# Attention softmax of a hybrid encoder trunk: logits and their minimum in one VectorE instruction, the mask added to the gates, 1/sum on VectorE, v transposed in another bank

## The chip, the cores and the metric

One core of one Trainium2 chip runs the whole program. The metric is the device time of one execution in microseconds (us), lower is better. The profile is of one execution, taken by the hardware profiler; its engines are PE (TensorE matmul; PEld is its weight load), DVE (VectorE), ACT (ScalarE), POOL (GpSimd) and SP (the queue that issues most of the transfers).

## What is computed

Two layers of a hybrid block run over 512 prompt tokens and 32 sample tokens. Each layer normalises x, multiplies it by one large input matrix, feeds three branches (a convolution module, retention, and forgetting attention, "FoX"), merges them with gates, and ends with a convolutional feed-forward block. The part that is changed is the attention:

```python
def fox_block(q, c_q, pos_q, k, v, c_k, pos_k):
    s = jnp.einsum('bthd,bshd->bhts', q, k) * (DH_FOX ** -0.5)
    bias = transpose(c_q)[..., :, None] - transpose(c_k)[..., None, :]   # cumulative log of the forget gate
    mask = pos_k[None, :] <= pos_q[:, None]
    s = jnp.where(mask[None, None], s + bias, -jnp.inf)
    p = jax.nn.softmax(s, axis=-1)
    return jnp.einsum('bhts,bshd->bthd', p, v)
```

There are 8 heads of 64. The prompt's 512 queries go in four blocks of 128; block qb sees (qb + 1) * 128 keys, the last 128 of them under a triangular mask. The sample's 32 queries see 256 cached keys and their own 32. The term c_q is the same for a whole row, so it drops out of a softmax over that row.

## The kernel before

**Matrix products.** Activations lie transposed (channels on partitions, 544 tokens along the row). A product by a large weight is three passes of matmuls of 272 columns (high part by high, high by low, low by high), accumulated in `acc` (pool psA, two buffers): L310, in `gemm`. One `slot` is one output tile of 128 channels: 48 such matmuls and an eviction by a callback, mostly `R_norm.evict` (L399, VectorE, `acc` times the norm). A weight block comes over the SP queue as `raw` (L195), is rounded into `hi` (L203, ScalarE), copied negated into `lo` (L206, ScalarE), and a GpSimd transfer that adds (L207) makes `lo` the remainder.

**What is woven in.** In the middle of a `gemm`, after 2/8, 4/8 and 6/8 of its passes, hooks call work that was put off (`later`), one step of the generators in `side` and some steps of those in `extra` (`tick`). `conv_side` is in `extra`: the depthwise convolution, one VectorE instruction of 574 columns a step (L486, then L488, 27 per channel tile, four tiles a layer), and products of ScalarE (L491) summed on GpSimd (L495). `fox_side` is in `side`: attention, 34 items (2 of the sample, then 32 of the prompt: head pairs, four query blocks each, even head then odd head). At step k item k computes its scores and softmax, item k-3 its transposes, item k-5 its product with v. A scheduler then orders each engine's instructions by when it reckons them ready, with earlier program text first, so that an engine's queue is not the program's order; on the chip each queue runs in the order so fixed.

**One item of the prompt.** Scores (L747, TensorE) of an even head and its mate go into the two buffers of psS at once. `c` is the row of cumulative gates of the head, broadcast to 128 partitions by a transfer (`ck`, L672, three buffers). L753 (VectorE) makes c - c_q - scores out of PSUM, L754 adds the mask on the last 128 columns, L680 takes the row's minimum, L682 (ScalarE) the exponential with its row sum, L684 (VectorE) the reciprocal, L685 (ScalarE) multiplies by it. Then four-fold transposes into the one buffer of psT (L761), their eviction (L763, ScalarE), and the products with v into the one buffer of psO (L779). The sample's two items do the same with L694, L700, L705, L706 and L712 to L731.

**Before it.** Just ahead of attention stand the slots of q (four), k (four) and v (four, `v_done`), then those of the retention's q and k, whose rotation reads a copy by transfers (L808), then L811 (GpSimd), L812 (VectorE) and L813 (GpSimd). q and k are normalised two slots after their product: `head_mean` multiplies by a block matrix into the two buffers of psS (L341, L342), and `rsqrt` reads them (L353 on ScalarE, L357 on VectorE). `v_done` transposes v, also two slots later: four transposes into a buffer of psS (L625), one into psT (L627), both evicted by ScalarE (L628, L629). The same callback serves the retention's v later in the layer, where the retention itself uses psO (L890).

## Time and profile before

| | |
|---|---|
| device time, median of 3 runs | 1995.84 us (1991.99 to 1999.47) |
| the profiled execution | 1999.15 us, of which the span from first to last instruction is 1997.0 us |
| PE busy | 1951.2 us (98%) |
| DVE busy | 950.5 us (48%) |
| ACT busy | 1062.5 us (53%) |
| POOL busy | 425.3 us (21%) |
| mean granted TensorE clock | 0.991 |

Each row of a group below is one line of the profile. In lists of instructions the columns are: line, engine, operation, output<-input by the program's names, output<-input shape, number; then busy time in us, the mean of one in ns; then the engine's idle time just before them in us and what released it. In a timeline a line begins with its start and its length in us, and the idle time before it stands in square brackets.

### The profile page before, as it was taken

The page shows a single profiled execution, that of the slowest core. Times are in us where ns is not written, and L with a number is a line of the kernel's source. Part 1 is how long each engine was busy: PE and PEld are TensorE (multiplying, and loading weights), DVE is VectorE, ACT ScalarE, POOL GpSimd, SP SyncE. Part 2 cuts the span into 40 slices and gives each one's busy share as a digit, 9 for nine tenths or more (in the row PEclk, how much of TensorE's full clock was granted, in tenths as well). Part 3 has the DMA queues.
Part 4 walks back from the last instruction along what each step waited for, and adds up shares of the span by engine and source line. Part 5 has one row for each costly group of instructions (what it writes and reads, how often), then busy time and mean ns, then how long its engine had stood idle before and what let it go on. Part 6 is the DMA issues. An engine that isn't in the chain of part 4 may idle for free.

```text
span 1997.0 us, 37750 instructions
## 1 busy us (share of the span) xinstructions
PE 1951.2 (98%) x15832; PEld 1909.6 (96%) x15832; DVE 950.5 (48%) x1641; ACT 1062.5 (53%) x1462; POOL 425.3 (21%) x580
## 2 busy tenths in 40 slices
PE   7999999999999999999999998999999999999999
PEld 6999889999999999999999987999999999999999
DVE  4377978555234330233224869784543343303330
ACT  5475664476455543454555666636654554434442
POOL 2142422121111221122112334121211122112211
PEclk8999999999999999999999999999999999999999
DMA  7786646567787787787987775556778877777786
GB/s 226 173 186 163 155 106 135 133 153 164 177 218 175 173 179 174 174 176 176 209 205 160 191 172 127 127 122 146 152 169 197 197 175 174 178 173 177 174 184 141
DMA packets 105717, 337.91 MB, mean 169 GB/s; under 512 B 17628, under 2 KB 19276, under 8 KB 105164
## 3 DMA queue, kind: packets, MB, share of 16 engines
q0 software_dynamic: 41760, 152.06, 45.6%
q1 hardware_dynamic: 63788, 183.44, 27.8%
q8 instruction: 124, 2.03, 0.4%
q14 instruction: 45, 0.37, 0.1%
HBM read 321.11 MB, written 9.89 MB: 166 GB/s over the span
## 4 chain that ended last, share of the span: by engine, by line
PE 80%; issue 6%; DVE 6%; ACT 2%; DMA 2%; POOL 2%; SPq 1%; DVEq 0%; POOLq 0%; ACTq 0%
PE acc L310 75%; DVE w L488 3%; DMA lo<-in_wpack_dram 1%; PE s L747 1%; DMA w<-q 1%; PE o L779 1%; DVE w L754 1%; PE t L761 1%; DVE w L753 1%; POOL lo L207 1%; DMA w<-cscr 0%; DVE mn L680 0%; POOL w L377 0%; ACT lo L206 0%; PE s L866 0%
## 5 line engine op out<-in xcount | busy, mean ns | idle before, releaser
L310 PE MATMUL acc<-q,hi 128*128 128x272 f32 x9344 | 1791.3, 291 | 12.7 <-ACT q L328 7.6
L310 PEld LDWEIGHTS acc<-q,hi 128*128 128x128 f32 x9344 | 1478.4, 190 | 27.1 <-ACT q L328 8.7
L310 PE MATMUL acc<-q,lo 128*128 128x272 f32 x4672 | 1352.2, 290 | 5.7 <-DMA lo<-in_wpack_dram 5.4
L310 PEld LDWEIGHTS acc<-q,lo 128*128 128x128 f32 x4672 | 884.4, 190 | 6.8 <-DMA lo<-in_wpack_dram 6.3
L203 ACT ACTIVATE hi<-raw 128x1024 fp32r<-128x1024 f32 (+1 forms) x293 | 309.8, 1057 | 655.5 <-PE acc L310 654.0
L207 POOL DMA_DIRECT2D lo<-in_wpack_dram x290 | 251.7, 868 | 1264.6 <-ACT lo L206 1174.9
L206 ACT ACTIVATE lo<-hi 128x1024 fp32r<-128x1024 f32 x290 | 305.1, 1052 | 4.4
L488 DVE SCALAR_TENSOR_TENSOR w<-w,par 128x574 f32<-128x574 f32 x208 | 198.4, 954 | 3.8
L1177 DVE TENSOR_TENSOR q<-acc,q 128x544 f32<-128x544 f32 x32 | 23.2, 725 | 218.6 <-PE acc L310 218.6
L399 DVE TENSOR_TENSOR w<-acc,R 128x544 f32<-128x544 f32 x94 | 67.7, 720 | 120.2 <-PE acc L310 118.4
L1136 DVE TENSOR_TENSOR w<-acc,R 128x32 f32<-128x32 f32 x44 | 8.5, 192 | 154.6 <-PE acc L310 154.1
L1144 DVE SCALAR_TENSOR_TENSOR w<-w,par 128x546 f32<-128x546 f32 x44 | 34.7, 788 | 83.5 <-ACT w L1143 83.5
L1146 ACT ACTIVATE w<-w 128x546 f32<-128x546 f32 x44 | 29.1, 662 | 70.5 <-DVE w L1145 70.5
L682 ACT ACTIVATE w<-w,mn 128x128 f32<-128x128 f32 (+4 forms) x68 | 37.7, 555 | 31.4 <-DVE mn L680 29.0
L326 DVE TENSOR_TENSOR q<-w,q 128x544 fp32r<-128x544 f32 x44 | 31.9, 725 | 33.7 <-ACT q L325 33.7
L335 DVE TENSOR_TENSOR wr<-w,wr 128x544 fp32r<-128x544 f32 x24 | 26.5, 1104 | 42.7 <-ACT wr L334 42.7
L495 POOL TENSOR_TENSOR w<-w 128x574 f32<-128x574 f32 x24 | 40.1, 1670 | 19.8 <-ACT w L491 19.2
L357 DVE SCALAR_TENSOR_TENSOR w<-s,w 128x272 f32<-128x272 f32 (+1 forms) x60 | 23.6, 435 | 43.4 <-ACT w L354 42.9
L1016 DVE SCALAR_TENSOR_TENSOR w<-w,acc 128x544 f32<-128x544 f32 x32 | 23.0, 720 | 43.6 <-PE acc L310 43.3
L685 ACT ACTIVATE w<-w,rs 128x128 f32<-128x128 f32 (+4 forms) x68 | 37.4, 554 | 9.6 <-DVE rs L684 9.2
L753 DVE SCALAR_TENSOR_TENSOR w<-ck,CM,s 128x128 f32<-128x128 f32 (+3 forms) x64 | 34.3, 536 | 13.4 <-PE s L747 13.4
L811 POOL TENSOR_TENSOR w<-w,cst 128x544 f32<-128x544 f32 x16 | 27.1, 1693 | 56.4 <-DMA w<-q 56.4
(203 smaller groups left out, 1434.7 us busy)
## 6 DMA issues: line engine op xcount, KB each, us to landing
raw<-in_wpack_dram SPq DMA_DIRECT2D x291, 512.0 KB, 3.4
lo<-in_wpack_dram POOLq DMA_DIRECT2D x290, 512.0 KB, 5.5
w<-in_x_dram SPq DMA_DIRECT2D x16, 272.0 KB, 5.2
out_dram<-w SPq DMA_DIRECT2D x16, 272.0 KB, 4.7
w<-q SPq DMA_DIRECT2D x64, 68.0 KB, 4.0
ck<-cscr SPq DMA_DIRECT2D x16, 256.0 KB, 4.2
xn<-q SPq DMA_DIRECT2D x8, 272.0 KB, 5.3
w<-xn SPq DMA_DIRECT2D x8, 272.0 KB, 5.8
```

The source lines that it names most:

```text
L203: act(hi[:, sl], self.raw[u][:, sl], AF.Copy)
L206: act(lo[:, sl], hi[:, sl].bitcast(F32), AF.Copy, scale=-1.0)
L207: nc.gpsimd.dma_start(lo[:, sl], wpack[u][:, sl], accum_op=ALU.add)
L310: mm(acc[:, h, :HN], w, half(x, h), start=(i == 0 and j == 0), stop=(i == n - 1 and j == len(passes) - 1))
L326: vtt(lo, src, hi.bitcast(F32), op=ALU.subtract)
L399: vtt(two(out), acc, two(self.R), op=ALU.mult)
L488: stt(c, u[:, k : k + CO], pcol(w + k), c, op0=ALU.mult, op1=ALU.add)
L495: gtt(p, p, t, op=ALU.add)
L682: act(L[:, :n], L[:, :n], AF.Exp, scale=-1.0, bias=mn, accum_out=sm)
L685: act(L[:, :n], L[:, :n], AF.Copy, scale=rs)
L753: stt(L[:, :n], c[:, :n], CM[:, h, qb : qb + 1], p[:, :n], op0=ALU.subtract, op1=ALU.subtract)
L1144: stt(c, a[:, 1 : 1 + FO], pcol(w + 1), c, op0=ALU.mult, op1=ALU.add)
```

## The change

Five things are altered, in `v_done`, `softmax`, `s_scores` and `p_scores`. (1) The attention's v is transposed into psO's buffer (the retention's v still into psS), and `vs` has one buffer in place of two. (2) The scale of q is negated, so that scores come out negative. (3) A new helper `ck_diag` adds the mask to the 128 gates of the diagonal block on GpSimd, into four buffers `cm`; it is called for the item at hand and for the same head's next query block, and at the end of a head pair for the next pair. (4) L753, L754 and L680 become one or two `tensor_tensor_reduce`: sum of gates and scores, and its minimum, on the columns before the diagonal block and then on the diagonal block with the first minimum as start; c_q is dropped. The sample's items keep their instructions. (5) The product with 1/sum goes from ScalarE (L685) to a VectorE `tensor_scalar`, for sample and prompt. The loads of `ck` are asked for earlier in the program.

```diff
-        def v_done(vt, vs, j, out):
+        def v_done(vt, vs, j, out, bank):
...
-                    t = psS_t()
+                    t = bank()
...
-        nc.vector.tensor_scalar(gq8, pcol(P_GQ), 0.125, None, op0=ALU.mult)
+        nc.vector.tensor_scalar(gq8, pcol(P_GQ), -0.125, None, op0=ALU.mult)
...
-        fvs = spool.tile([P, 512], F32, tag="vs", name="vs")
+        fvs = spool.tile([P, 512], F32, tag="vs", name="vs", bufs=1)
         for j in range(4):
-            slot(rhs, v_done(fv, fvs, j, o_fv[l]))
+            slot(rhs, v_done(fv, fvs, j, o_fv[l], psO_t))
...
+            def ck_diag(h, qb):
+                if h < 8 and (h, qb) not in ckm:
+                    t = wpool.tile([P, P], F32, tag="cm", name="cm", bufs=4)
+                    gtt(t, ck(h)[:, qb * P : (qb + 1) * P], cmask, op=ALU.add)
+                    ckm[h, qb] = t
+                return ckm.get((h, qb))
...
-            def softmax(L, n):
-                mn = spool.tile([P, 1], F32, tag="mn", name="mn", bufs=4)
-                nc.vector.tensor_reduce(mn, L[:, :n], axis=AX.X, op=ALU.min)
+            def softmax(L, n, mn=None):
+                if mn is None:
+                    mn = spool.tile([P, 1], F32, tag="mn", name="mn", bufs=4)
+                    nc.vector.tensor_reduce(mn, L[:, :n], axis=AX.X, op=ALU.min)
...
-                act(L[:, :n], L[:, :n], AF.Copy, scale=rs)
+                nc.vector.tensor_scalar(L[:, :n], L[:, :n], rs, None, op0=ALU.mult)
...
-                stt(L[:, :n], cks[g], cqs[:, g : g + 1], p[:, :n], op0=ALU.subtract, op1=ALU.subtract)
+                stt(L[:, :n], cks[g], cqs[:, g : g + 1], p[:, :n], op0=ALU.subtract, op1=ALU.add)
...
-                stt(L[:, :n], c[:, :n], CM[:, h, qb : qb + 1], p[:, :n], op0=ALU.subtract, op1=ALU.subtract)
-                vtt(L[:, n - P : n], L[:, n - P : n], cmask, op=ALU.add)
-                softmax(L, n)
+                m = ck_diag(h, qb)
+                if qb < 3:
+                    ck_diag(h, qb + 1)
+                mn = [spool.tile([P, 1], F32, tag="mn" + x, name="mn", bufs=4) for x in "ab"]
+                at = BIG
+                for x, o, e, t in ((c[:, : n - P], 0, n - P, mn[0]), (m, n - P, n, mn[1])):
+                    if e > o:
+                        nc.vector.tensor_tensor_reduce(L[:, o:e], x, p[:, o:e], 1.0, at, ALU.add, ALU.min, t)
+                        at = t
+                softmax(L, n, mn[1])
+                if qb == 1 and h % 2 and h < 7:
+                    ck(h + 1)
+                if qb == 3 and h % 2 == 0 and h < 6:
+                    ck(h + 3)
+                if qb == 3 and h % 2 and h < 7:
+                    ck_diag(h + 1, 0)
+                    ck_diag(h + 2, 0)
```

## Rows read from the trace of the kernel before

**Rows 1.** The first part of the profile's page: busy time of each engine, share of the span, instructions.

```profile
span 1997.0 us, 37750 instructions
PE 1951.2 (98%) x15832; PEld 1909.6 (96%) x15832; DVE 950.5 (48%) x1641; ACT 1062.5 (53%) x1462; POOL 425.3 (21%) x580
```

**Rows 2.** The waits of the PE alone, over the span: line, what it waited for, us in total, number, longest.

```profile
PE s L747 <- DVE w L753: 5.8, 4, 3.0
...
PE t L761 <- ACT w L763: 5.1, 4, 1.9
PE s L625 <- DVE w L357: 4.2, 2, 2.1
...
PE t L712 <- ACT w L717: 1.6, 2, 0.9
PE s L694 <- DVE w L705: 0.8, 2, 0.4
```

**Rows 3.** Stretches by time (us from the span's start): length, then busy time of PE, PEld, DVE, ACT, POOL with the number of instructions, then the granted TensorE clock (1.00 is full), the DMA share and GB/s. The first five are the stretches right behind a wait of the PE; the last is one in which VectorE is full.

```profile
147.50:151.50 4.00, 4.00 (x20) 4.00 (x21) 3.96 (x7) 1.39 (x3) 1.01 (x3) 0.57 1.06 274
1133.30:1137.30 4.00, 4.00 (x23) 4.00 (x24) 3.96 (x7) 1.39 (x3) 0.96 (x2) 0.65 1.05 274
181.20:185.60 4.40, 4.38 (x21) 4.01 (x22) 2.24 (x6) 2.34 (x8) 2.44 (x3) 0.61 0.82 142
256.90:260.50 3.60, 3.55 (x17) 3.55 (x18) 3.60 (x7) 0.49 (x1) 0.99 (x1) 0.55 0.74 179
1209.20:1212.80 3.60, 3.58 (x15) 2.89 (x16) 3.60 (x9) 2.39 (x7) 1.96 (x1) 0.55 0.96 207
...
214.00:262.00 48.00, 42.62 (x343) 37.42 (x343) 47.45 (x86) 29.61 (x63) 21.52 (x15) 0.96 0.57 132
```

**Rows 4.** Timeline of the first layer in the slots of v, by engine: first VectorE (two lines hold several instructions of the convolution), then the first v's transposes on TensorE and their eviction on ScalarE; last, two slots of 48 matmuls from the chain of waits, as a measure of an undisturbed slot (start, length, what).

```profile
141.42 5.67 DVE L488 SCALAR_TENSOR_TENSOR w<-w,par 128x574 f32<-128x574 f32 x2
147.01 0.78 DVE L357 SCALAR_TENSOR_TENSOR w<-s,w 128x272 f32<-128x272 f32 x2
149.07 0.71 DVE L399 TENSOR_TENSOR w<-acc,R 128x544 f32<-128x544 f32 x1
150.40 6.14 DVE L488 SCALAR_TENSOR_TENSOR w<-w,par 128x574 f32<-128x574 f32 x6
156.46 0.72 DVE L399 TENSOR_TENSOR w<-acc,R 128x544 f32<-128x544 f32 x1
...
147.50 0.66 PE L625 MATMUL s<-cst,w 128*128 128x128 f32 x4 [2.10 <-DVE w L357]
...
148.19 0.60 ACT L628 ACTIVATE q<-s 128x512 f32<-128x512 f32 x1 [1.82 <-PE s L625]
...
97.97 6.01 PE acc L310 x48
104.48 6.00 PE acc L310 x48
```

**Rows 5.** VectorE's instructions of the softmax and of the convolution over the whole span, by shape.

```profile
L753 DVE SCALAR_TENSOR_TENSOR w<-ck,CM,s 128x128 f32<-128x128 f32 x16 | 5.4, 337 | 2.2 <-PE s L747 2.2
L753 DVE SCALAR_TENSOR_TENSOR w<-ck,CM,s 128x256 f32<-128x256 f32 x16 | 7.5, 472 | 4.1 <-PE s L747 4.1
L753 DVE SCALAR_TENSOR_TENSOR w<-ck,CM,s 128x384 f32<-128x384 f32 x16 | 9.6, 602 | 4.8 <-PE s L747 4.8
L753 DVE SCALAR_TENSOR_TENSOR w<-ck,CM,s 128x512 f32<-128x512 f32 x16 | 11.8, 735 | 2.2 <-PE s L747 2.2
L754 DVE TENSOR_TENSOR w<-w,cst 128x128 f32<-128x128 f32 x64 | 29.2, 456 | 0.8
L680 DVE TENSOR_REDUCE mn<-w 128x1 f32<-128x128 f32 x16 | 4.5, 279 | 0.3
...
L680 DVE TENSOR_REDUCE mn<-w 128x1 f32<-128x512 f32 x16 | 10.8, 677 | 0.1
L486 DVE TENSOR_SCALAR w<-w,par 128x574 f32<-128x574 f32 x8 | 4.6, 570 | 0.0
```

**Rows 6.** Single lines of the program: number, shortest/median/longest in ns, first and last start.

```profile
L639 DVE TENSOR_SCALAR gq<-par x2: 154/154/154, 5.4 to 31.2; 128x1 f32<-128x1 f32 x2
L754 DVE TENSOR_TENSOR w<-w,cst x64: 266/284/1495, 175.7 to 1270.0; 128x128 f32<-128x128 f32 x64
L682 ACT ACTIVATION_READ_ACCUMULATOR w<-w,mn x68: 184/188/192, 172.6 to 1274.3; 128x1 f32 x68
L685 ACT ACTIVATE w<-w,rs x68: 385/528/726, 173.3 to 1275.5; 128x128 f32<-128x128 f32 x16, 128x256 f32<-128x256 f32 x16, 128x384 f32<-128x384 f32 x16, 128x512 f32<-128x512 f32 x16
```

**Rows 7.** One group of GpSimd's instructions, in the stretch from 174.6 to 265 us alone.

```profile
L811 POOL TENSOR_TENSOR w<-w,cst 128x544 f32<-128x544 f32 x8 | 13.4, 1672 | 29.6 <-DMA w<-q 29.6
```

**Rows 8.** Timelines of VectorE (first three lines: one mask addition, and the first and last logits of the prompt in the first layer) and of GpSimd (the other two), at the same clock of the trace.

```profile
211.15 1.28 DVE L754 TENSOR_TENSOR w<-w,cst 128x128 f32<-128x128 f32 x1
...
175.27 0.35 DVE L753 SCALAR_TENSOR_TENSOR w<-ck,CM,s 128x128 f32<-128x128 f32 x1 [0.70 <-PE s L747]
...
285.46 0.73 DVE L753 SCALAR_TENSOR_TENSOR w<-ck,CM,s 128x512 f32<-128x512 f32 x1
...
178.06 1.90 POOL L811 TENSOR_TENSOR w<-w,cst 128x544 f32<-128x544 f32 x1 [7.40 <-DMA w<-q]
...
210.93 1.36 POOL L813 TENSOR_TENSOR q<-q,w 128x544 f32<-128x544 f32 x1
```

More of the change, by code (lines that the diff above doesn't have):

```diff
@@ L674, in ck @@
                 return ckp[h]
+            ckm = {}
+            def ck_diag(h, qb):
[4 more added lines that the diff above has]
+                return ckm.get((h, qb))
             yield
-            def softmax(L, n):
-                mn = spool.tile([P, 1], F32, tag="mn", name="mn", bufs=4)
-                nc.vector.tensor_reduce(mn, L[:, :n], axis=AX.X, op=ALU.min)
+            def softmax(L, n, mn=None):
+                if mn is None:
+                    mn = spool.tile([P, 1], F32, tag="mn", name="mn", bufs=4)
+                    nc.vector.tensor_reduce(mn, L[:, :n], axis=AX.X, op=ALU.min)
                 sm = spool.tile([P, 1], F32, tag="sm", name="sm", bufs=4)
@@ L1031, in branch @@
                     if m == 0:
-                        rvt.extend((vtile(), spool.tile([P, 512], F32, tag="vs", name="vs")))
-                    slot(rhs, v_done(rvt[0], rvt[1], m, None))
+                        rvt.extend((vtile(), spool.tile([P, 512], F32, tag="vs", name="vs", bufs=1)))
+                    slot(rhs, v_done(rvt[0], rvt[1], m, None, psS_t))
                 elif kind == "r":
```

## The prediction, made before the changed kernel ran

> **What bounds the kernel now.** The page comes first: TensorE is busy for 98% of the span, no other engine for much over half [rows 1]. So nothing done on VectorE, ScalarE or GpSimd shortens the kernel in itself; only time in which TensorE waits, or runs at its lower clock, can come back. The list of TensorE's waits says how much that is and which part of it this change touches [rows 2]: scores that wait for the logits to be read out of psS (5.8 us), transposes that wait for psT's eviction (5.1), v's transposes that wait for psS (4.2), and the sample's items (1.6 and 0.8): 17.5 us.
>
> To that belongs what follows a wait. The stretches behind the five longest stops show a granted clock of 0.55 to 0.65 [rows 3], the engine being at the lower of its two levels (1.2 in place of 2.4 GHz) for most of them. At clock g a stretch of t us loses (1 - g) t: 1.7 and 1.4 us behind v's two waits, 1.7 behind the sample's, 1.6 and 1.6 behind two of attention's, 8.0 us in all. Together 25.5 us of 1997 hang on waits that the change touches. That is the most it can give by this way, and it is 1.3%.
>
> Behind attention's waits stands VectorE. It is busy 47.45 of 48 us in the stretch of the first layer where they fall [rows 3], and the second layer's is alike; the convolution's instructions are packed into whatever other work leaves, six in a row between two evictions of v [rows 4], so a logit that is ready still queues.
>
> **v into psO.** What goes is the wait for psS, which k's last normalisation holds until its two reads (L357, from 147.01) are through [rows 4]; in front of them a pair of convolution instructions took 5.67 us. psO has no reader at that time: its next user, the sample's product with v, stands behind all four slots of v. So 4.2 us of waiting and 3.1 us of clock are at stake, 7.3. What is late next: with 2.1 us won the last v slot is done at about 157.1 (the transposes begin at 145.4 and take 0.66, three quarters of a slot of 6.0 us follow, then one whole slot at a pitch of 6.5 [rows 4]), while the third v is evicted only from 156.46 to 157.18 [rows 4], and the slot after needs that buffer. The v before it is evicted by 149.78, ahead of the 150.6 at which its buffer is wanted. I keep 0.4 us a layer for that: **-6.5 us**. That four v tiles now share one buffer costs nothing: a slot lies between two of them and the eviction takes 0.60 us [rows 4]. vs in one buffer costs nothing either: the sample is first in attention and the retention's first write comes when attention's 110 us [rows 8] are over; without that distance it would be one wait for an eviction.
>
> **The sample's start.** The 0.8 us of L694 come from psS shared with v's transposes, and go with them. The 1.6 us of L712 wait for an eviction on ScalarE behind other work, L685 among it. Of these and the 1.7 us of clock behind the first I take half: **-2.4 us** with the 0.8.
>
> **Softmax on VectorE.** What is removed, from the busy times of [rows 5]: L753 34.3, L754 29.2, L680 30.6 (64 at the mean of its smallest and largest, as its time grows evenly with the columns), together 94.1 us in both layers. What is added: the new instruction reads the same columns, in pieces. No row shows it; its nearest is L753, which also adds a row in SBUF to PSUM. In 16 items of each size that is 128; 128+128; 256+128; 384+128 columns: four pieces of 128 and one each of 128, 256, 384, at 337, 337, 472, 602 ns, thus 16 x 2.76 = 44.1 us. If the minimum is read out by an instruction of its own, as ScalarE's row sum is (188 ns [rows 6]), 112 of these add 21 us; L680 writes its minimum with no such row, and I take zero. The product with 1/sum: between 154 ns for one column [rows 6] and 570 for 574 [rows 5] lie 246, 340, 430 and 520 ns for the four sizes, 24.6 us; the other end is one column at a time as in L680, 30.6 us. The reciprocal stays. So VectorE is relieved by 94.1 - 44.1 - 24.6 = 25 us, 19 with the slow product, about nothing with readouts as well.
>
> **The mask on GpSimd.** 64 additions of 128 columns are new. L811 has 544 in 1.67 us [rows 7]; by columns that is 0.39, and with a fixed part like that of VectorE's L680 (279 ns for 128 where a quarter of 677 is 169 [rows 5]) 0.50: 25 to 32 us on an engine that is busy for 21% [rows 1]. But it meets VectorE: L754 takes 0.28 us in the median and up to 1.5 [rows 6], and the one of 1.28 us starts at 211.15 while GpSimd's L813 runs from 210.93 to 212.29 [rows 8]. L753, with one operand in PSUM, shows no such spread between its sizes [rows 5]. The Trainium skill, page "SBUF — State Buffer", section "Who interferes with whom", has this as an exclusive lock: a VectorE instruction with two SBUF inputs and a GpSimd instruction that reads SBUF exclude each other, and a tensor_scalar in its two-port mode excludes any GpSimd work. The trace agrees on the first with those two rows (1.28 against 0.28 us); on the second no run here shows anything yet. By the rule the new logits are out of it and the 64 additions and 68 products are in it, which is the second rival below.
>
> I let half of the additions' time fall on VectorE. The 32 items of a layer take 110 us [rows 8], 3.5 each, so the 48 us of [rows 3] hold some 13: 13 x 0.39 (25 us over 64) = 5.1 us of relief, less 13 x 0.45 / 2 = 2.9, so 2.2 us net. VectorE's lateness there is what the 5.8 us of score waits measure, 2.9 a layer; 2.2 a layer of it goes: -4.4.
>
> **ScalarE.** L685 goes, 68 at a median of 528 ns, 36 us over both layers [rows 6]. In 13 items that is 6.9 us off a queue in which L763, the eviction that transposes wait for, stands behind it. Of its 5.1 us I take half, -2.5; the other half waits for VectorE through the exponential. The 3.2 us of clock behind these waits I leave where they are, since a remaining short wait has lowered the clock too (0.91 us did at 181.2) [rows 2, 3]. Attention's part is **-6.9 us**.
>
> **Edits at nothing.** The sign of q's scale is one instruction on one column. The broadcasts of ck are as many as before, asked for earlier; where one waits for its buffer it now stands ahead of rotation copies and weight loads on SP, for at most the one item whose logits release it, 3.5 us. Weights are asked for three blocks ahead (`ahead`), which covers it; without that cover each of 8 such loads could put off a slot by it.
>
> **Sum.** -6.5 - 2.4 - 6.9 = -15.8 us. Against the profiled execution (1999.15 us, 2.15 of it outside its span) that is 1983.4; that execution lies 3.3 above the median of the runs, and against the median it is 1980.0. I forecast 1980 us. About 0.5%, 10 us, is what a measurement of this kernel can tell from no change: the line lies at 1985.9.
>
> **Rivals.** *All waits go.* VectorE's relief of 25 us and ScalarE's of 36 are larger than what is waited for, so the queues may empty: 25.5 us, 1970. Against it: VectorE is full because convolution work is moved up into its gaps, and that will fill new gaps as well. 0.10.
>
> *VectorE stays full.* The additions on GpSimd shut out the products and the convolution as L813 shut out L754, and for their whole length: 64 x 0.45 = 29 us at most, as much as the relief of 19 to 25. Readouts of the minimum would do the same. Then attention's waits stay and only v's 6.5 and the 0.8 us of the sample go: -7.3, about 1988 to 1989, no change that can be told. For it speaks the 5.67 us of two convolution instructions in [rows 4]; against it that L754, which collides today, goes. 0.25.
>
> *The mask comes late* (slower). GpSimd's queue is in order, and L811 sits at its head waiting for a rotation's copy: 29.6 us in eight times, once 7.4 [rows 7, 8]. An addition that is queued behind it waits that, 1.9 for L811 and 1.4 for L813, up to 10.7 us; its lead is two items, 7.1 us. It is then up to 3.6 us late, say 2.5, and behind it stand the logits on VectorE, psS and the next scores on TensorE. Of 16 rotations six eat the whole gain; with ten it is 25 - 16 = +9 us, 2005. Against it: additions depend only on ck, which lies there long before, so they are likely put ahead. 0.13.
>
> *No effect at all*, if every wait only changes its name: 1996, 0.02.
>
> **How the numbers follow.** The forecast has 0.50, by itself from 1974 (-22) to 1987 (-9, v's part and the start alone). Of its chance 0.40 lies below 1985.9 and 0.10 within the line. All waits gone: 0.10 faster. VectorE full: 0.05 faster, 0.20 within. Late mask: 0.11 slower, 0.02 within. No effect: 0.01 within, 0.01 slower. Faster 0.55, same 0.33, slower 0.12. The range from 1969 to 1999 holds the first rival's 1970 and the no-effect case; the slower rival and the ends of the unknown costs beyond it are left out, some 0.15 to 0.2.
>
> **What would show it.** Right: v's transposes with no wait and the full clock behind them (the old places are 147.5 and 1133.3 us); no L685 on ScalarE; VectorE's softmax at 69 us in place of 94; score and transpose waits together at 4 to 5 us. The forecast is wrong if new instructions on 128 columns take clearly more than 0.34 us, if a readout row follows them, if the convolution's mean of instructions rises, or if VectorE idles in front of logits with GpSimd named as releaser.

## The result: 2008 us in place of 1994, slower by 0.6%

The changed kernel takes 2008.1 us (median of 4 runs, 2005.6 to 2010.5), the kernel before 1993.9 beside it: a ratio of 1.0063, 95% interval 1.0043 to 1.0084. The forecast of 1980, and the sign, were wrong. The profiled execution took 2007.24 us.

The first part of its page answers to [rows 1]:

```profile
span 2005.3 us, 37930 instructions
PE 1953.3 (97%) x15832; PEld 1909.1 (95%) x15832; DVE 947.1 (47%) x1741; ACT 1031.5 (51%) x1394; POOL 461.6 (23%) x644
```

ScalarE has lost 31 us and GpSimd gained 36, as planned. VectorE, which was to lose 25, has lost 3.4.

The waits of the PE over the span (line, what it waited for, us in total, times, longest) answer to [rows 2]:

```profile
PE acc L310 <- DMA lo<-in_wpack_dram: 11.5, 3, 5.3
PE s L758 <- DVE mn L772: 11.0, 6, 5.5
...
PE t L787 <- ACT w L789: 6.9, 8, 2.4
```

The 4.2 us of v's transposes and the 2.4 of the sample's start are gone from the list. But scores wait 11.0 us where 5.8 were, transposes 6.9 where 5.1 were, and two new waits, for the low part of a weight, stand in the slots of v (3.29 and 2.94 us; the old one, of 5.4 us, is elsewhere). All rows of the list together are 47.4 us, where they were 41.0.

Stretches behind the longest new waits, in the columns of [rows 3]:

```profile
152.50:157.00 4.50, 4.47 (x23) 4.47 (x24) 4.36 (x7) 0.74 (x2) 0.84 (x1) 0.62 1.02 224
231.00:236.00 5.00, 4.44 (x16) 3.69 (x17) 3.57 (x13) 1.85 (x5) 0.79 (x2) 0.52 0.46 125
1143.00:1147.50 4.50, 4.33 (x19) 4.33 (x20) 4.39 (x6) 0.91 (x3) 0.88 (x1) 0.50 1.03 217
```

As before, the granted clock is low behind these waits (0.50 is the lower of its two levels, 1.2 GHz, for a whole stretch), so such a wait costs more than its own length.

**The slots of v.** The timeline of GpSimd, and the PE's wait in it:

```profile
139.52 1.76 POOL L682 TENSOR_TENSOR cm<-ck,cst 128x128 f32<-128x128 f32 x2 [3.50 <-DMA ck<-cscr]
141.25 1.95 POOL L495 TENSOR_TENSOR w<-w 128x574 f32<-128x574 f32 x1
143.16 1.88 POOL L682 TENSOR_TENSOR cm<-ck,cst 128x128 f32<-128x128 f32 x2
144.99 0.87 POOL L207 DMA_DIRECT2D lo<-in_wpack_dram  x1
...
148.37 1.18 POOL L207 DMA_DIRECT2D lo<-in_wpack_dram  x1
...
152.53 0.48 PE L310 MATMUL acc<-q,lo 128*128 128x272 f32 x1 [3.29 <-DMA lo<-in_wpack_dram]
```

GpSimd's queue also issues the transfers that make a weight's low part (L207). Four additions of the mask now stand ahead of them, the first after 3.50 us of waiting for the gates; the two issues come 2.2 and 1.7 us later than before, where they were at 142.78 and 146.67.

**The softmax.** VectorE's instructions by shape, which answer to [rows 5], and GpSimd's additions:

```profile
L488 DVE SCALAR_TENSOR_TENSOR w<-w,par 128x574 f32<-128x574 f32 x208 | 199.0, 957 | 3.9
L772 DVE CUSTOM_DVE_ANT_0 w<-cm,s,mn 128x128 f32<-128x128 f32 x48 | 16.3, 340 | 2.6
L696 DVE TENSOR_SCALAR w<-w,rs 128x512 f32<-128x512 f32 x16 | 11.0, 689 | 0.3
...
L772 DVE DVE_READ_ACCUMULATOR2_ANT mn<- 128x1 f32 x112 | 8.9, 80 | 0.0
L772 DVE CUSTOM_DVE_ANT_0 w<-ck,s 128x384 f32<-128x384 f32 x16 | 8.7, 543 | 4.2 <-PE s L758 4.2
...
L696 DVE TENSOR_SCALAR w<-w,rs 128x128 f32<-128x128 f32 x16 | 7.8, 484 | 0.4
...
L682 POOL TENSOR_TENSOR cm<-ck,cst 128x128 f32<-128x128 f32 x64 | 42.1, 667 | 51.8 <-DVE mn L772 30.0 <-DMA ck<-cscr 20.5 <-DVE rs L695 1.0
```

The new instruction takes 0.28 to 0.34 us for 128 columns and 0.54 for 384, 40.4 us in all, and behind each of the 112 stands a readout, a row of 80 ns (`DVE_READ_ACCUMULATOR2_ANT`) that writes the minimum. These rows add up to 8.9 us, but they lie beside other instructions: 55 of the 112 start in the same nanosecond as the instruction behind them (227.56 in the next timeline), and only 0.9 of the 8.9 us lie beside no other row of VectorE. The product takes 484 ns in the mean for 128 columns and 274 at its shortest.

**The longest stall.** VectorE, GpSimd and PE in layer 0:

```profile
227.22 0.41 DVE L772 CUSTOM_DVE_ANT_0 w<-ck,s 128x256 f32<-128x256 f32 x1
227.56 0.07 DVE L772 DVE_READ_ACCUMULATOR2_ANT mn<- 128x1 f32 x1
227.56 3.67 DVE L488 SCALAR_TENSOR_TENSOR w<-w,par 128x574 f32<-128x574 f32 x1
231.16 0.33 DVE L772 CUSTOM_DVE_ANT_0 w<-cm,s,mn 128x128 f32<-128x128 f32 x1
...
231.90 0.81 DVE L488 SCALAR_TENSOR_TENSOR w<-w,par 128x574 f32<-128x574 f32 x1
...
227.64 1.70 POOL L495 TENSOR_TENSOR w<-w 128x574 f32<-128x574 f32 x1
228.99 1.62 POOL L837 TENSOR_TENSOR w<-w,cst 128x544 f32<-128x544 f32 x1
...
231.56 1.22 PE L758 MATMUL s<-q 64*128 64x512 f32 x2 [5.54 <-DVE mn L772]
```

An item's logits are now two instructions, and the second needs the first's minimum. Between them stands here an instruction of the convolution, as it does in 14 of the 48 split items; it takes 3.67 us, with two GpSimd instructions running beside it, where the next one takes 0.81. Until the second piece has read them, the scores keep their bank (their buffer in PSUM), and TensorE stands. Before, the first instruction (L753) read all the scores, and no hold was over 0.75 us; now the 48 split items hold their bank 1.32 us in the mean and 4.27 at most, from the first piece's start to the second's end.

### The profile page after: what moved, and what is told of

It reads as the page before. It is cut to its first block, busy times and chain, and to the rows that moved or that the text cites. A ratio compares the mean times of both kernels' runs of the same rounds, so it can differ in the third digit from the quotient of the medians.

```text
span 2005.3 us, 37930 instructions
## 1 busy us (share of the span) xinstructions
PE 1953.3 (97%) x15832; PEld 1909.1 (95%) x15832; DVE 947.1 (47%) x1741; ACT 1031.5 (51%) x1394; POOL 461.6 (23%) x644
## 4 chain that ended last, share of the span: by engine, by line
PE 78%; issue 6%; DVE 5%; DMA 4%; ACT 2%; POOL 2%; SPq 1%; DVEq 0%; POOLq 0%; ACTq 0%
PE acc L310 74%; DVE w L488 2%; DMA w<-q 2%; DMA lo<-in_wpack_dram 2%; PE o L805 1%; DVE w L772 1%; DVE w L696 1%; PE s L758 1%; PE t L787 1%; SPq L834 1%; POOL lo L207 1%; DMA w<-cscr 0%; PE s L892 0%; ACT hi L203 0%; PE o L916 0%
## 5 line engine op out<-in xcount | busy, mean ns | idle before, releaser
L207 POOL DMA_DIRECT2D lo<-in_wpack_dram x290 | 251.7, 868 | 1237.6 <-ACT lo L206 1175.4
L488 DVE SCALAR_TENSOR_TENSOR w<-w,par 128x574 f32<-128x574 f32 x208 | 199.0, 957 | 3.9
L682 POOL TENSOR_TENSOR cm<-ck,cst 128x128 f32<-128x128 f32 x64 | 42.1, 667 | 51.8 <-DVE mn L772 30.0
L789 ACT ACTIVATE w<-t 128x128 f32<-128x128 f32 (+3 forms) x64 | 27.4, 428 | 31.4 <-PE t L787 25.9
L758 PE MATMUL s<-q 64*128 64x256 f32 (+2 forms) x192 | 31.1, 364 | 11.0 <-DVE mn L772 11.0
```

Of the source, the lines that this page charges most:

```text
L207: nc.gpsimd.dma_start(lo[:, sl], wpack[u][:, sl], accum_op=ALU.add)
L488: stt(c, u[:, k : k + CO], pcol(w + k), c, op0=ALU.mult, op1=ALU.add)
L682: gtt(t, ck(h)[:, qb * P : (qb + 1) * P], cmask, op=ALU.add)
L758: mm(ps[e][:, :nn], qhl[a][own, h // 2, NS + qb * P : NS + n], khl[b][own, h // 2, NS : NS + nn], start=(i == 0), stop=(i == 2))
```

## The experiments

Theories at the start: (A) the additions on GpSimd cost the time, in its queue and by shutting VectorE out; (B) the product on VectorE does; later (D) the split of the logits into two pieces does, by holding the scores' bank or by making the minimum late. Ratios are to the kernel before, run beside each; where two runs are compared in us below, it is by the difference of their ratios times 1994 us, as the kernel before ran between 1993.7 and 1995.7 beside them. An edit also lets the scheduler order the engines' queues anew. By line and shape every queue of e1 has the order of the kernel before, and the queues of VectorE, ScalarE and TensorE in e2 have that of the changed kernel; in the other runs the order of VectorE's queue, at least, has moved with the edit.

| run | us (median) | ratio, 95% interval |
|---|---|---|
| changed kernel | 2008.1 | 1.0063 (1.0043 to 1.0084) |
| e1 v alone | 1992.0 | 0.9988 (0.9977 to 0.9998) |
| e2 no additions | 2008.3 | 1.0068 (1.0054 to 1.0083) |
| e3 additions on VectorE | 2004.0 | 1.0040 (1.0025 to 1.0055) |
| e4 product on ScalarE | 2004.3 | 1.0055 (1.0035 to 1.0074) |
| e5 one piece | 1990.2 | 0.9974 (0.9965 to 0.9984) |
| e6 independent pieces | 2016.7 | 1.0115 (1.0100 to 1.0129) |
| e7 as e6, product on ScalarE | 2002.8 | 1.0049 (1.0034 to 1.0063) |
| e8 one piece, product on ScalarE | 1996.2 | 1.0000 (0.9987 to 1.0014) |
| e9 one piece, mask in place | 1994.3 | 0.9999 (0.9987 to 1.0011) |
| e10 one piece, idle second | 1986.9 | 0.9949 (0.9931 to 0.9967) |
| e11 one piece, late minimum | 1998.9 | 1.0019 (1.0007 to 1.0030) |
| e12 mask by TensorE, fp32r | 2018.9 | 1.0112 (1.0088 to 1.0135) |
| e13 changed kernel, longer lag | 2004.8 | 1.0054 (1.0034 to 1.0074) |
| e14 as e9, longer lag | 1998.8 | 1.0021 (1.0008 to 1.0034) |
| e15 mask by TensorE, bf16 | 2004.1 | 1.0043 (1.0027 to 1.0059) |
| e16 as e9, mask on VectorE | 1993.6 | 0.9997 (0.9986 to 1.0008) |
| e17 as e10, second waited for | 1996.8 | 1.0005 (0.9994 to 1.0017) |
| e18 as e11, not waited for | 1992.2 | 0.9991 (0.9981 to 1.0002) |

**e1: v's part alone.** Only `v_done` and its calls are changed; `vs` keeps its two buffers.

```diff
-                    t = psS_t()
+                    t = bank()          # psO_t in attention, psS_t in retention
```

> The kernel before with one edit: attention's v is transposed into psO. Theory A (the psS wait of 2.1 us a layer goes, but TensorE then reaches the next weight block before its remainder has landed; in the changed kernel that wait was 3.3 and 2.9 us, with GpSimd's additions ahead of the transfer, and by the old places of L207 about 1.2 us of it stays without them): 3 to 5 us faster than before, v's transposes without a wait and a wait for lo of 1 to 2 us a layer in their place. Rival (nothing takes its place): 7 us faster, no wait for lo in the slots of v. Rival (all of it is given back): no difference.

It gains 0.12% (0.02 to 0.23), about 2 us. v's wait is gone and no wait for a weight takes its place, but scores now also wait for the sample's logits. PE waits of e1:

```profile
PE t L761 <- ACT w L763: 6.9, 5, 1.9
...
PE s L747 <- DVE w L753: 4.7, 4, 1.8
...
PE s L747 <- DVE w L705: 2.9, 4, 0.8
```

**e2: no additions.** The mask on the prompt is left out.

```diff
...
-                    gtt(t, ck(h)[:, qb * P : (qb + 1) * P], cmask, op=ALU.add)
-                    ckm[h, qb] = t
+                    ckm[h, qb] = ck(h)[:, qb * P : (qb + 1) * P]
```

> The changed kernel without GpSimd's 64 additions: the diagonal block's logits take the gates unmasked, so the mask on the prompt is left out. Theory A (the additions cost it: they lock VectorE out and hold up GpSimd's queue): at least 18 us faster than the changed kernel and 5 to 12 us faster than before; score waits under 4 us, the product with 1/sum near its undisturbed 280 to 490 ns. Theory B (the product with 1/sum on VectorE costs it): within 5 us of the changed kernel. Theory C (the two-piece instruction with its readouts costs it): within 5 us of the changed kernel, score waits still near 11 us.

Theory A falls: the time stays, and so does the stall of 5.54 us at 231. The waits for weights in the slots of v go, 6.2 us; but attention's clock is lower instead (0.93 from 170 to 300 us, where the changed kernel has 0.96), and TensorE, which reaches attention earlier, waits more there for other things (its list has 45.7 us in all, the changed kernel's 47.4). A second way from logits to TensorE is seen here, in layer 0 (VectorE, ScalarE, PE):

```profile
197.67 0.73 DVE L836 TENSOR_TENSOR q<-q,cst 128x544 f32<-128x544 f32 x1 [2.90 <-DMA w<-q]
198.31 0.55 DVE L770 CUSTOM_DVE_ANT_0 w<-ck,s 128x384 f32<-128x384 f32 x1
...
199.29 0.72 ACT L691 ACTIVATE w<-w,mn 128x512 f32<-128x512 f32 x1 [4.91 <-DVE mn L770]
...
200.96 0.47 ACT L787 ACTIVATE w<-t 128x384 f32<-128x384 f32 x1
...
201.48 0.55 PE L785 MATMUL t<-cst,w 128*128 128x128 f32 x3 [2.83 <-ACT w L787]
```

The logits stand on VectorE behind a rotation that waits 2.90 us for its copy. The exponential waits 4.91 us for the minimum at the head of ScalarE's queue, and behind it, and behind one rounding of a weight, waits the eviction (L787) that frees a bank for the next transposes.

**e3: additions on VectorE.**

```diff
-                    gtt(t, ck(h)[:, qb * P : (qb + 1) * P], cmask, op=ALU.add)
+                    vtt(t, ck(h)[:, qb * P : (qb + 1) * P], cmask, op=ALU.add)
```

> The changed kernel with the 64 additions on VectorE in place of GpSimd; nothing is left out. Theory A (GpSimd's queue and the lock): 10 to 18 us faster than the changed kernel, near or a little below before (1984 to 1994), since VectorE takes back 18 us of work. Rival (VectorE's sum of work decides, wherever the additions stand): as slow as the changed kernel or slower.

**e4: product on ScalarE.**

```diff
-                nc.vector.tensor_scalar(L[:, :n], L[:, :n], rs, None, op0=ALU.mult)
+                act(L[:, :n], L[:, :n], AF.Copy, scale=rs)
```

> The changed kernel with the product with 1/sum back on ScalarE. Theory A (the additions cost it): at most 5 us faster than the changed kernel, score waits above 7 us. Theory B (the product on VectorE costs it, 37 us of VectorE's time of which 12 are lock): at least 10 us faster than the changed kernel, near before.

Both lie within the changed kernel's interval or just below it: e3 is 5 us faster than the changed kernel, e4 2 us, and neither difference is clear of the intervals. Neither gives the loss back, so theories A and B both miss.

**e5: one piece.** e2 with one instruction over all columns (mask left out).

```diff
-                for x, o, e, t in ((c[:, : n - P], 0, n - P, mn[0]), (m, n - P, n, mn[1])):
-                    ...
+                nc.vector.tensor_tensor_reduce(L[:, :n], c[:, :n], p[:, :n], 1.0, BIG, ALU.add, ALU.min, t)
```

> The changed kernel with the logits and their minimum in one instruction over all columns, against the gates without mask: the additions on GpSimd are gone and the mask on the prompt is left out. It differs from the run without additions (2008.3 us) only in that the bank of the scores is freed by one instruction and not by the second of two. Theory D (the second piece, behind a convolution instruction, frees the bank late): 1993 to 1999 us, the wait of scores for the logits at 6 us or less and the 5.5 us stall at 231 gone, the two layers' stages 8 to 14 us shorter in sum than 408.4. Rival (the product on VectorE is what costs): 2004 to 2008, stages within 4 us of it.

It is 19 us faster than e2, from which the program differs by the split alone: without the split the loss against the kernel before (13 us) is more than given back. What the split costs includes the order of instructions that the scheduler makes of it. The same stretch of attention, first in e2, then in e5 (columns of [rows 3]):

```profile
170.00:300.00 130.00, 117.23 (x924) 103.36 (x922) 91.76 (x246) 66.14 (x145) 41.15 (x32) 0.93 0.53 120
```

```profile
170.00:300.00 130.00, 123.67 (x1037) 110.98 (x1037) 99.31 (x215) 70.77 (x153) 46.74 (x35) 0.99 0.61 138
```

With one piece the PE has 1037 rows of matmuls there in place of 924, at a clock of 0.99, and VectorE is busier, not idler.

**e6 and e7: independent pieces.** Both pieces start from BIG, and a one-column instruction takes the lesser minimum; e7 also has e4's edit.

```diff
...
-                        nc.vector.tensor_tensor_reduce(L[:, o:e], x, p[:, o:e], 1.0, at, ALU.add, ALU.min, t)
+                        nc.vector.tensor_tensor_reduce(L[:, o:e], x, p[:, o:e], 1.0, BIG, ALU.add, ALU.min, t)
+                if qb:
+                    vtt(mn[1], mn[0], mn[1], op=ALU.min)
```

> The changed kernel with two pieces that don't depend on one another: both minima start from the large constant, and a small VectorE instruction on one column takes the lesser (48 more instructions). Nothing is left out. Theory D: the pieces can stand back to back and the bank is freed 0.8 us or more earlier; 1999 to 2004 us, the 5.5 us stall at 231 gone. Rival (the product costs, or the number of instructions): 2008 to 2012, stages as before or longer than 409.9 us in sum.

> The same with the product with 1/sum back on ScalarE. Nothing is left out. Theory D and the product's cost add up: 1992 to 1998 us. Rival (either explains the loss alone): as the better of the two single edits, 2003 to 2004 for the product alone (2004.3 measured).

In e6 the bank of a split item is freed after 0.72 us in the mean, and the time is 10 us longer still than the changed kernel's, outside both expectations; the longest stall of scores is 5.2 us, so that is not gone either. A shorter hold in the mean does not bring the time back. e7 is near e4, as its rival had it.

**e8: one piece, product on ScalarE** (e5 with e4's edit).

> Logits in one instruction and the product on ScalarE; the mask on the prompt is left out, with no additions anywhere. Theory D with a cost of the product besides: the fastest of the four, 1983 to 1990 us, below the 1992 of the kernel before with v's transposes moved, since VectorE then has neither the minimum nor the mask's addition. Rival (the fused instruction or its readout is itself the cost): 1994 or more.

A miss: 5 us slower than e5. With one piece, the product is better on VectorE.

**e10, e11, e17, e18: which of the split's effects.** All are e5 (mask left out) with one VectorE instruction more in 48 items. e10 reads the scores as the second piece does; e11 passes the minimum through a one-column instruction. e17 is e10, and e18 is e11, with the one dependency turned round.

```diff
 e10   nc.vector.tensor_tensor_reduce(L[:, :n], c[:, :n], p[:, :n], 1.0, BIG, ALU.add, ALU.min, t)
+                if qb:
+                    nc.vector.tensor_tensor_reduce(z, c[:, n - P : n], p[:, n - P : n], 1.0, t, ALU.add, ALU.min, u)
 e17
+                    t = u
 e11
+                if qb:
+                    vtt(u, t, t, op=ALU.min)
+                    t = u
 e18
-                    t = u
```

> The one-piece run (mask on the prompt left out, 1990.2 us) with a second instruction added back in 48 items: it reads the last 128 columns of the scores and the first one's minimum as the split's second piece does, but what it writes is read by nobody. So the scores' bank is held, and VectorE is loaded, as with the split (20 us more work), while the exponential waits for the first instruction alone. If the hold of the bank is the cost: 2003 to 2010, with a stall of scores of several us. If the later minimum is the cost: 1990 to 1995.

> The one-piece run (mask left out, 1990.2 us) with a VectorE instruction on one column behind the logits in 48 items, through which the minimum passes on its way to the exponential. The bank is freed by the one instruction as before; the minimum takes a second trip through VectorE's queue. If the later minimum is the cost: 2000 to 2010, with longer waits of transposes for the eviction. If the hold of the bank is: 1990 to 1995.

> The run with an idle second piece (one piece, mask left out, a second instruction on the last 128 columns in 48 items: 1986.9 us) with one thing changed: the exponential takes the second instruction's minimum in place of the first's, so it waits for it. Instructions and work are the same. If the later minimum is the cost: 2000 to 2010, thus +13 to +23 from this one dependency. If it explains only what e11 showed (+8.7): 1994 to 1998. If other things made the loss of the split: 1985 to 1990.

> The run with a late minimum (a VectorE instruction on one column behind the logits in 48 items, mask left out: 1998.9 us) with one thing changed: nobody waits for that instruction. If lateness of the minimum is the cost: 1987 to 1992, like the one-piece run without it. If the number of instructions on VectorE is: 1996 to 2001.

e10 holds the bank 1.26 us in the mean, as long as the changed kernel does (1.32), and its 48 more instructions and their readouts are 20 us of rows (VectorE is busy for 947.7 us, in e5 for 937.7). It is the fastest of all, 5 us below e5 and faster than either expectation. In the program both e10 to e17 and e18 to e11 change nothing but what the exponential waits for, and cost 11 us (0.9949 to 1.0005) and 6 us (0.9991 to 1.0019). The scheduler's order moves with it: from e10 to e17 some 67 of VectorE's 1629 instructions stand elsewhere, from e18 to e11 some 44, and some of ScalarE's and TensorE's too. So what is measured is the dependency together with the order that is built around it, not the wait alone. PE waits of e10, of e17 and of e11:

```profile
PE s L756 <- DVE mu L768: 3.5, 6, 1.1
PE t L782 <- ACT w L784: 3.3, 3, 1.9
```

```profile
PE s L756 <- DVE mu L768: 6.6, 5, 5.3
PE t L783 <- ACT w L785: 5.8, 6, 1.6
```

```profile
PE t L782 <- ACT w L784: 12.4, 6, 3.8
...
PE s L756 <- DVE mn L764: 4.8, 3, 4.2
```

In e17 a stall of 5.3 us is back, with the scene of the changed kernel. From VectorE and GpSimd:

```profile
221.88 3.54 DVE L488 SCALAR_TENSOR_TENSOR w<-w,par 128x574 f32<-128x574 f32 x1
225.34 0.33 DVE L768 CUSTOM_DVE_ANT_0 cm<-ck,s,mn 128x128 f32<-128x128 f32 x1
...
221.82 1.69 POOL L495 TENSOR_TENSOR w<-w 128x574 f32<-128x574 f32 x1
223.18 1.62 POOL L833 TENSOR_TENSOR w<-w,cst 128x544 f32<-128x544 f32 x1
```

Over both layers, from the start of the logits to the end of the product, 9 of the 64 items take over 6 us in the changed kernel (longest 9.2), 9 in e2 (10.1), 9 in e17 (7.7) and 5 in e11 (10.1), but 1 in e5 (6.4) and in e18 (6.01) and none in e10 (6.0). Between these kernels late items go with lost time. In the kernel before, 10 take over 6 us (7.9), and its items take 4.8 us in the mean where the changed kernel's take 3.6, with no such loss; so neither the count nor the mean length sets the time by itself.

**e13: a longer lag for the changed kernel.**

```diff
-                for lag, f in ((3, 1), (5, 2), (0, 0)):
+                for lag, f in ((4, 1), (6, 2), (0, 0)):
```

> The changed kernel whole, with TensorE taking an item's transposes four steps behind its scores in place of three, and its product with v six behind in place of five. The chain from logits to product (up to 9.2 us in layer 0 of the changed kernel) then has 3.5 us more before anyone waits for it. If late chains are what costs: the 6.9 us of waits of transposes mostly go, those of scores for the logits stay, and the time is 1996 to 2003. If VectorE's load, the hold of the bank or the order of the convolution costs: 2005 to 2011.

PE waits of e13:

```profile
PE s L758 <- DVE mn L772: 10.3, 6, 4.0
...
PE t L787 <- ACT w L789: 1.7, 5, 0.5
```

The transposes' waits go as expected and the scores' stay, but the time lies between the two expectations, and its interval contains the changed kernel's 1.0063. No gain from the longer lag is shown, so lateness towards the transposes is at most a small share of the loss.

**e9, e14, e16, e12, e15: whole versions with one piece.** e9 takes the query blocks from the last to the first, so that the mask can be added to the gates in place; e14 is e9 with e13's lag, e16 has the additions on VectorE. In e12 and e15 TensorE adds the mask.

```diff
 e9
+            def ck_mask(h, qb):
+                b = ck(h)[:, qb * P : (qb + 1) * P]
+                gtt(b, b, cmask, op=ALU.add)                  # e16: vtt
 ...
-                for qb in range(4):
+                for qb in (3, 2, 1, 0):
 ...
 e12 and e15
 ...
+                            if i == 0:
+                                mm(ps[e][:, n - P : n], idr, mskr, start=False, stop=False, skip_group_check=True)
```

> A whole version: the logits and their minimum in one instruction; each head's query blocks are taken from the last to the first, so that GpSimd can put the mask onto the gates in place (block qb - 1 after the logits of block qb have read it). Theory D (only the split costs): 1986 to 1994 us, like the run with one piece and no mask (1990.2), faster than the changed kernel by 14 or more. Rival (the additions matter once the split is gone, or they come late because each waits for the logits before it): 1998 to 2006, with GpSimd named as the releaser of logits.

> The whole version with one piece, blocks from the last to the first and the mask in place on GpSimd (1994.3 us), with the same longer lag. Its chains reach 8.1 us. If late chains still cost there, 1987 to 1991, below both kernels; if not, 1993 to 1997.

> The whole version with one piece and blocks from the last to the first, with the additions of the mask on VectorE in place of GpSimd (64 x 0.28 us more there, 42 us fewer on GpSimd, which shuts VectorE out). By the run with an idle second piece, in which 20 us more on VectorE cost nothing: 1988 to 1994, at or below the 1994.3 with GpSimd. If an addition lies in the chain of the next logits: 1996 to 2002.

> A whole version: logits in one instruction, the mask added to the scores by TensorE (64 matmuls of 128 columns more, identity by mask). Theory D: 1990.2 us of the one-piece run and 64 x 0.06 us of matmul, by a 272-column matmul's pitch of 0.12, so 1992 to 1997. Rival: above 2000 if the longer matmul group makes the scores late.

> The whole version with the mask added by TensorE, with identity and mask in bf16 in place of fp32r (64 matmuls took 330 ns each, 21.1 us in all, in the run with fp32r, and the time was 2018.9). If a bf16 matmul of 128 columns takes as long as a column a cycle at the high clock, some 0.06 us, it is 2018.9 less about 15 to 25, thus 1992 to 2002, and about 1994 if it is the one-piece run (1990.2) plus 64 x 0.06.

e9 and e16 give the split's loss back and come out level with the kernel before: the mask on either engine, with the other order of the blocks, costs the 5 us by which they lie above e5. The longer lag costs e9 4 us. The mask by TensorE was a miss in both runs; its matmul in e12, then in e15:

```profile
L762 PE MATMUL s<-mskr,idr 128*128 128x128 f32 x64 | 21.1, 330 | 0.0
```

```profile
L763 PE MATMUL s<-mskr,idr 128*128 128x128 bf16 x64 | 14.7, 230 | 0.0
```

Their length is not the whole price. In e5 the first score matmuls of the two heads of a pair, of 64 rows each, start within some 5 ns of one another (six in 0.89 us from 273.22 us on); in e12 the mask's matmul stands between them, they start 0.69 us apart, and the group takes 2.04 us (from 293.24). For 32 pairs that is 37 us, an estimate from these two groups, of the order of the 28 us by which e12 lies above e5, where e12 had been expected at 64 x 0.06 us.

Of the whole versions only e1 is faster than both kernels: 0.9988 of the one, with an interval that just excludes 1, and 15 us below the other.

## Why the prediction was wrong

**v into psO** (-6.5): the direction was right, the size was not. Alone (e1, with every queue in its old order) it is worth about 2 us (0.02 to 0.23%), though the wait went as described; scores and transposes behind it wait longer (L761 6.9 us for 5.1, and 2.9 us new for the sample's logits). The trace from which the waits were read is of an execution of 1999.15 us, 5 us above the median of the 25 beside e1, so a part of the size may lie there; no run shows how large a part. In the changed kernel two new waits for weights (6.2 us) stand where v's stood. That is the step "edits at nothing": it counted the queue of SP and held that weights are asked for early enough. The queue that mattered was GpSimd's, where additions stand ahead of the issue of the low parts. But it does not explain the loss: e2 has neither the additions nor these waits and is no faster.

**The sample's start** (-2.4): the waits of 1.6 and 0.8 us are gone from the changed kernel's list, but not for the reasons given. e2, e3, e5, e10, e11, e17 and e18, all without L685 on ScalarE and without the additions on GpSimd, each still have 1.2 us of the transposes' wait, and scores there wait for the sample's logits. From e2's list:

```profile
PE s L756 <- DVE w L714: 1.8, 3, 0.8
PE t L721 <- ACT w L726: 1.2, 2, 0.6
```

That they are missing just where TensorE is held up by weights before points to those waits as what hid them; it is luck, not the forecast's relief.

**Softmax on VectorE** (relief of 25 us): the logits were right, 40.4 us against 44.1. The readouts, which the text bounded at 21 and took as zero, are 8.9 us of rows that overlap others but for 0.9, so zero was nearly right. What was too small is the product, 36.8 us against 24.6 for the four sizes. By rows the relief is 94.1 - 40.4 - 8.9 - 36.8 = 8.0 us. The busy time fell by 3.4 only; the sample's products add 1.5, and the instructions of L602, one of which takes 4.03 us at 145.27 beside two of GpSimd, take 6.5 us longer than before, while overlaps go the other way. The Trainium skill, page "VectorE: DVE Perf Modes", section "Two Vector instructions with no wait between them", says that an operation which also writes out its accumulator is two instructions; the 112 readout rows agree.

**The mask on GpSimd**: 0.45 us undisturbed, in the range of 0.39 to 0.5; 0.67 in the mean. For the second half of the rule on the exclusive lock, which the prediction took from the page "SBUF — State Buffer" of the Trainium skill, section "Who interferes with whom", there was no row of the product then. Now there is, in e2:

```profile
226.44 3.22 DVE L694 TENSOR_SCALAR w<-w,rs 128x384 f32<-128x384 f32 x1
...
226.45 1.70 POOL L495 TENSOR_TENSOR w<-w 128x574 f32<-128x574 f32 x1
227.80 1.62 POOL L835 TENSOR_TENSOR w<-w,cst 128x544 f32<-128x544 f32 x1
```

The product of the same size at 194.35 takes 0.42 us; this one ends after both GpSimd instructions. With that the trace agrees with the rule's second half too.

**The step that failed** is the price of attention's part: "VectorE's lateness there is what the 5.8 us of score waits measure, 2.9 a layer; 2.2 a layer of it goes: -4.4". It priced the new logits by VectorE's busy time, and counted the split as columns in pieces (128+128, 256+128, 384+128); that the second piece depends on the first, that other work can get in between, that the bank is freed only by the second, and that the exponential waits for it, it put at nothing. The split costs 19 us (e2 against e5). Score waits rose by 5.2 us in place of falling by 4.4. VectorE's busy time is not the price: e10 has 20 us more of rows than e5 and is not slower. Of the parts of the split, the hold of the bank alone costs nothing (e10), and letting the exponential wait for a second instruction, with the order that goes with it, costs 11 and 6 us (e10 to e17, e18 to e11).

**ScalarE** (-2.5): L685 went, but the exponential now waits longer for the minimum at the head of the queue, first before, then after:

```profile
ACT w L682 <- DVE mn L680: 29.0, 26, 3.2
ACT w L693 <- DVE mn L772: 54.5, 40, 6.9
```

With one piece the part is real: e5 is 5 us faster than e8.

**The signs.** Of the signs of being right, v's transposes have no wait, L685 is gone, and the clock behind the first of them is full (1.00 from 143.76 to 147.76 us); but it is low behind the waits for weights that follow (0.62 and 0.50), VectorE's softmax has 86 us of rows and not 69, and score and transpose waits are 17.9 us and not 4 to 5. Of the four signs of being wrong only the readout row came: the pieces of 128 columns stay at 0.34 us, the convolution's mean went from 954 to 957 ns, and VectorE never idles in front of logits with GpSimd as releaser. The list of signs did not have the cause in it.

**The rivals.** "The mask comes late", at 2005, is nearest in time, and that is luck: e2 has no additions and takes 2008.3. "VectorE stays full" had a shut-out product and the readout rows come true, and misses the loss.

**What stays open.** The split costs 19 us (e5 to e2, 0.9974 to 1.0068). The later minimum, at equal instructions, makes 6 to 11 of it, together with the order that the scheduler builds around it. e17, which has the late minimum and a bank held still longer (1.50 us), is still 13 us faster than e2. In the profiled executions about half of this shows as waits of the PE (45.7 us in all in e2, 39.8 in e17), and the clock is lower besides (0.93 against 0.97 from 1165 to 1290 us); which instruction's place brings them is not traced, and neither is the excess of e6. Nor is it shown that the number of VectorE instructions in a row sets the time: the kernel before has three ahead of each exponential (L753, L754, L680), each waiting for the one in front, and does not have the loss. And that e10 is 5 us faster than e5, with more to do, shows that small edits move the time by several us for reasons not traced here; the 6 us from e18 to e11 are hardly more than that.

## What to carry to other kernels

What fusing saves can be lost again if the fused instruction must be cut in two that depend on each other: on a shared in-order queue something long can get in between, and whoever waits for the second waits for that too. The engine's busy time does not show this price; here 20 us more of it cost nothing, and one dependency cost 6 to 11 us. Measure it with a pair of kernels that do the same work and differ in who waits, and compare their queues' order before calling the wait the cause. And when work is moved to an idle engine, read first what else its queue issues: here it was the transfers of the weights, which came 2 us later.

## What the runs showed of the hardware that was not expected

- A VectorE instruction beside two GpSimd instructions in a row can take more than four times its time: L488 3.67 us, with rows of GpSimd of 1.70 and 1.62 us beside it, where the next L488 takes 0.81.
- A minimum accumulated by the fused instruction shows as a row of 80 ns behind it, while `tensor_reduce` writes its minimum with none; but 55 of 112 such rows start together with the instruction behind them, and they add next to nothing to the busy time.
- A matmul of 128 by 128 inside a group of fp32r matmuls has a row of 330 ns in fp32r and 230 in bf16, and the next matmul starts 0.26 and 0.16 us after it (medians). Put between two matmuls of 64 rows that otherwise start together, it also takes their overlap.
